# Second MLP product of a two-layer encoder written as seven block products, with one float32 arena for its raw weights

## Chip, core and metric

The kernel runs on one core of one Trainium2 chip. The metric is the device time of one execution in microseconds (us); the kernel before has three such times, 1996.44, 1997.36 and 1997.35, median 1997.35. The profile is one further execution of 1997.37 us, whose span from first to last instruction is 1995.5 us.

## What is computed

Two encoder layers on 512 tokens of width 1024, all float32. The attention mixers of a layer are left out here; the change touches what follows them:

```python
# per layer, after the first LayerNorm; h is (512, 1024)
f = jnp.square(jax.nn.relu(h @ w_ff1))                 # (512, 4096)
gate = jax.nn.sigmoid(h @ w_ple_gate)                  # (512, 1024)
u = alpha * h + f @ w_ff2 + gate * (p @ w_ple)
h = layer_norm(u, ln2_g, ln2_b)
```

Every product is made of three matrix products of rounded parts: each float32 operand is written as hi + lo, hi being a copy rounded to the matmul's type (fp32r) and lo the remainder, and the product is hi·hi + lo·hi + hi·lo.

## The kernel before

Weights arrive in chunks of 128 x 1024 float32 (512 KB), in the order in which `plan_layer` lists them. `take(key)` hands out the next chunk and first calls `ahead`, which issues loads on the SP queue (`load`, L142, two raw buffers), and splits chunks a few places ahead of their use (`split_next`, L152): ScalarE (ACT) copies raw to hi (L106), GpSimd (POOL) subtracts to get lo (L170). hi and lo live in an arena `R` of 64 slots of 128 x 512; 16 of them hold the hi and lo of h. `manual_schedule` keeps every engine's instructions in the order in which the program emits them, so an instruction that waits holds up all that stand behind it on its engine.

The MLP runs in three groups of 12, 12 and 8 inner tiles (`FF_GROUPS`). For each inner tile j of a group 24 matmuls (128 x 128 stationary, 128 x 512 moving) make 128 rows of the hidden layer for all 512 tokens in one PSUM bank. Then ACT takes relu (L1291), VectorE (DVE) squares (L1293), ACT copies to hi (L106) and DVE subtracts to lo (L109). After a group, `outer` makes its part of the second product, for each half f of the 1024 columns: four PSUM banks, one for each 128 tokens; each chunk of `w_ff2` holds two inner tiles and costs 4 x 6 matmuls. At the end of a half DVE adds the four banks into the rows `FD` (L1305, or L1303 with the factor alpha).

```python
            for c in range(4):
                n = 0
                for li, wi in SEQ3:
                    for k in range(2):
                        P.mm(P.PS[:, bs[c], :], xs(c, li, 2 * i + k), ww[k][wi], i == 0 and n == 0,
                             i == len(keys) - 1 and n == 5)
                        n += 1
```

Ahead of the MLP stands `outer` for the first column half of the gate product (chunks `pg` 0, tensor `in_wPG`), behind it the second half: there the four `pg` chunks are all taken first, and each 128 tokens then make 24 matmuls that run through all four chunks' hi before any lo. The gains g and b of the second LayerNorm (`gb`) are loaded on POOL's queue just ahead of these. LayerNorm itself is two DVE instructions on 128 x 1024 (L301, L303), and `ln_T` transposes its result on the PE (L97) for the next layer.

## Time and profile before

| what | before |
|---|---|
| median of three runs | 1997.35 us |
| the profiled execution, its span | 1997.37 us, 1995.5 us |
| PE (matmul) busy | 1954.3 us, 98%, 9440 instructions |
| DVE, ACT, POOL busy | 777.1, 755.2, 840.3 us |
| PE's share of the chain that ended last | 66% |

PE is the matmul engine, PEld its weight loads (they run beside the matmuls). Times in rows are us unless marked ns. A row of the timeline begins with the start and the length; `x` is a count, and what stands in brackets is the engine's idle time before it and what ended that. `PEclk` is the granted clock of TensorE as a share of 2.4 GHz.

### The profile page before, as it was taken

Reading aid. Unit: us, or ns where it says so; the run is one execution under the profiler, and the core shown is the slowest. Engines: PE = TensorE matmul, PEld = TensorE weight load, DVE = VectorE, ACT = ScalarE, POOL = GpSimd, SP = SyncE. Lnnn points to the kernel's source line nnn. Section 1 sums busy time; section 2 is a strip of 40 time slices with the busy share of each in tenths; the row PEclk is TensorE's granted clock in tenths of the full one; section 3 lists DMA queues with packets and bytes.
Section 4 is the critical chain, followed back from the end, with each engine's and each line's share of the span. In section 5 each row is a group of like instructions: output and inputs, shape, how many; then the busy total and the mean of one; then the engine's idle time right before and its main releaser. Section 6 shows DMA issues by size and latency. Waiting matters only on the chain.

```text
span 1995.5 us, 24072 instructions
## 1 busy us (share of the span) xinstructions
PE 1954.3 (98%) x9440; PEld 1611.4 (81%) x9440; DVE 777.1 (39%) x1565; ACT 755.2 (38%) x1313; POOL 840.3 (42%) x407
## 2 busy tenths in 40 slices
...
GB/s 168 108 54 82 99 112 97 89 82 61 147 117 95 96 126 74 107 87 103 122 111 68 57 82 103 82 125 72 101 56 168 96 102 101 102 84 127 67 120 78
DMA packets 59697, 195.96 MB, mean 98 GB/s; under 512 B 6720, under 2 KB 11968, under 8 KB 59584
## 3 DMA queue, kind: packets, MB, share of 16 engines
...
## 4 chain that ended last, share of the span: by engine, by line
PE 66%; DVE 3%; ACT 1%; POOL 1%; DMA 1%; issue 1%; DVEq 0%; ACTq 0%; POOLq 0%
PE PS L94 64%; PE PS L97 2%; ACT R L106 1%; POOL R L170 1%; DVE R L109 1%; DMA raw<-in_wO_dram 0%; DMA raw<-in_wPL_dram 0%; DVE gate L1254 0%; DVE FD L303 0%; DVE FD L301 0%; DVE p L394 0%; ACT p L386 0%; DVE qf L916 0%; DVE ysum L421 0%; DVE rt L915 0%
## 5 line engine op out<-in xcount | busy, mean ns | idle before, releaser
L94 PE MATMUL PS<-R 128*128 128x512 f32 (+4 forms) x8528 | 1886.2, 378 | 12.3 <-DVE R L365 5.3
L94 PEld LDWEIGHTS PS<-R 128*128 128x128 f32 (+1 forms) x8528 | 1508.5, 187 | 333.0 <-issue 37.6
L170 POOL TENSOR_TENSOR R<-raw,R 128x1024 fp32r<-128x1024 f32 (+1 forms) x304 | 734.7, 2421 | 848.5 <-ACT R L106 811.2
L106 ACT ACTIVATE R<-raw 128x1024 fp32r<-128x1024 f32 x306 | 321.1, 1053 | 340.8 <-PE PS L94 143.5
L106 ACT ACTIVATE R<-PS 128x128 fp32r<-128x128 f32 (+5 forms) x300 | 131.7, 450 | 131.9 <-PE PS L97 82.3
L109 DVE TENSOR_TENSOR R<-PS,R 128x512 fp32r<-128x512 f32 (+5 forms) x276 | 134.4, 494 | 118.7 <-ACT R L106 117.5
L1109 POOL TENSOR_TENSOR M<-M,gate 128x512 f32<-128x512 f32 x48 | 62.1, 1293 | 191.7 <-DVE gate L1108 135.5
L386 ACT ACTIVATE p<-p,s 128x256 f32<-128x256 f32 (+2 forms) x96 | 66.1, 688 | 187.1 <-DVE s L551 65.4
L1293 DVE TENSOR_TENSOR ff<-relu 128x512 f32<-128x512 f32 x64 | 44.3, 692 | 222.1 <-ACT relu L1291 222.1
L1305 DVE TENSOR_TENSOR FD<-FD,PS 128x512 f32<-128x512 f32 x40 | 27.5, 687 | 242.5 <-PE PS L94 242.5
L1291 ACT ACTIVATE relu<-PS 128x512 f32<-128x512 f32 x64 | 38.3, 599 | 168.5 <-PE PS L94 168.5
L394 DVE TENSOR_SCALAR p<-p,s 128x512 f32<-128x512 f32 (+3 forms) x128 | 95.0, 742 | 4.5
L97 PE MATMUL PS<-ident,p 128*128 128x128 f32 x480 | 73.6, 273 | 2.8 <-DVE p L394 1.7
L97 PEld LDWEIGHTS PS<-ident,p 128*128 128x128 f32 x480 | 58.6, 140 | 16.1 <-DVE p L394 2.5
L109 DVE TENSOR_TENSOR R<-ff,R 128x512 fp32r<-128x512 f32 x64 | 44.3, 692 | 47.6 <-ACT R L106 47.6
L1108 DVE SCALAR_TENSOR_TENSOR gate<-gate,PS 128x512 f32<-128x512 f32 x48 | 32.9, 686 | 71.1 <-ACT gate L1104 42.8
L106 ACT ACTIVATE R<-ff 128x512 fp32r<-128x512 f32 x64 | 40.5, 632 | 50.9 <-DVE ff L1293 50.9
L393 DVE RECIPROCAL s<-s 128x1 f32<-128x1 f32 x128 | 20.9, 163 | 79.3 <-ACT p L386 78.1
L277 POOL TENSOR_TENSOR s<-s,mhalf 128x1 f32<-128x1 f32 x18 | 21.4, 1192 | 71.9 <-DVE s L275 71.9
L627 DVE CUSTOM_DVE_ANT_0 p<-PS,bd 128x512 f32<-128x512 f32 x32 | 21.8, 682 | 76.1 <-PE PS L94 76.1
L386 ACT ACTIVATE p<-PS,s 128x512 f32<-128x512 f32 x32 | 22.0, 689 | 53.2 <-DVE s L481 53.0
L106 ACT ACTIVATE R<-M 128x512 fp32r<-128x512 f32 (+3 forms) x20 | 13.8, 695 | 62.3 <-POOL M L1109 52.7
...
## 6 DMA issues: line engine op xcount, KB each, us to landing
raw<-in_wF_dram SPq DMA_DIRECT2D x128, 512.0 KB, 3.4
raw<-in_wT_dram SPq DMA_DIRECT2D x106, 512.0 KB, 3.5
raw<-in_wBR_dram SPq DMA_DIRECT2D x16, 512.0 KB, 3.5
raw<-in_wO_dram SPq DMA_DIRECT2D x16, 512.0 KB, 3.6
raw<-in_wPG_dram SPq DMA_DIRECT2D x16, 512.0 KB, 3.4
raw<-in_wVD_dram SPq DMA_DIRECT2D x12, 512.0 KB, 3.4
hsp<-FD SPq DMA_DIRECT2D x8, 512.0 KB, 6.1
FD<-hsp SPq DMA_DIRECT2D x8, 512.0 KB, 5.9
```

What stands on the lines that cost most here:

```text
L94: self.nc.tensor.matmul(out, l, r, start=start, stop=stop, skip_group_check=True)
L97: self.nc.tensor.transpose(out, in_, self.ident)
L106: self.nc.scalar.activation(out=out, in_=in_, func=AF.Copy, scale=scale)
L109: self.nc.vector.tensor_tensor(out=out, in0=a, in1=hi.bitcast(F32), op=ALU.subtract)
L170: nc.gpsimd.tensor_tensor(out=lo, in0=raw, in1=hi.bitcast(F32), op=ALU.subtract)
L386: P.nc.scalar.activation(out=pt[:, 0:n], in_=src, func=AF.Exp, bias=nm, scale=1.0, accum_out=den)
L394: nc.vector.tensor_scalar(out=pt[:, 0:n], in0=pt[:, 0:n], scalar1=rd, scalar2=0.5, op0=ALU.mult, op1=ALU.mult)
L1108: nc.vector.scalar_tensor_tensor(out=t, in0=t, scalar=1.0, in1=pb, op0=ALU.add, op1=ALU.mult)
L1109: nc.gpsimd.tensor_tensor(out=P.M[:, j, :], in0=P.M[:, j, :], in1=t, op=ALU.add)
L1291: nc.scalar.activation(out=r, in_=ps, func=AF.Relu)
L1293: nc.vector.tensor_tensor(out=f, in0=r, in1=r, op=ALU.mult)
L1305: nc.vector.tensor_tensor(out=u, in0=u, in1=ps, op=ALU.add)
```

## The change

Two inner tiles (a pair), two halves of the tokens (256 each) and two halves of the columns (512 each) make a 2 x 2 by 2 x 2 block product A·W, which Strassen's scheme in Winograd's form does with seven block products instead of eight:

- left operands: a11, a12, a22, S1 = a21 + a22, S2 = S1 − a11, S3 = a11 − a21, S4 = a12 − S2;
- right operands: the four blocks of the raw weights, T1 = w12 − w11, T2 = w22 − T1, T3 = w22 − w12, T4 = T2 − w21, formed in place in the raw buffers by DVE (L196), so each T must wait until the block that it overwrites has been split;
- each right operand, 128 x 512, is now a chunk of its own: an ACT copy to hi and a POOL subtraction to lo (L201), seven in place of two chunks of 128 x 1024 per pair;
- products in the order P1, P5, P6, P2, P3, P7, P4, for all pairs of a group each; three pairs of PSUM banks X, Y, Z. P6 and P7 add to what P1 left in X, P3 to Y and P4 to Z. DVE adds X, Y or Z into `FD` after each product (L1434, L1436), so these running sums never need a further addition: P1's X must have been read before P6 goes on with it.

A product of one pair is 2 token tiles x 3 matmuls. The hidden tiles are made two at a time (`hidden`): two relu, two squares, then one split of the raw blocks, four additions on 128 x 256, one split of 128 x 1024 and one of 128 x 256. The 16 pairs of a layer go in groups of 2, 3, 3, 3, 3, 2; the first pair of the next group is made just ahead of a group's products. All former float32 buffers become one tile `F` of 39 units of 128 x 256; outside the MLP two raw buffers stay, inside it there is room for seven, and both raw halves of a pair stay from P1 until T3 or T4 have been split. Loads go up to four chunks ahead in place of two (`depth`). From P6 of the last group on, all but the two are closed again.

```diff
+U_P, U_PG, U_YS, U_RAW, N_UNIT = 16, 25, 29, 31, 39
...
-        self.M = const.tile([128, 8, 512], F32, name="M")
+        self.F = const.tile([128, N_UNIT, 256], F32, name="F")
+        self.M = self.F[:, 0:16, :].rearrange("p (a b) c -> p a (b c)", b=2)
+        self.pt = [self.units(U_P + 3 * i, 3) for i in range(3)]
+        self.pi = 0
+        self.ysum = self.units(U_YS, 2)
+        self.pg = self.units(U_PG, 4).rearrange("p (c t) -> p c t", c=4)
+        self.fa = Arena(N_UNIT)
+        self.fa.close(0, U_RAW)
...
-            self.load(self.cs + 2)
+            self.load(self.cs + self.depth)
...
+            if c['src'] is None:
+                self.cd += 1
+                continue
             if self.cd < 4:
                 c['raw'] = self.M[:, 2 * self.cd:2 * self.cd + 2, :].rearrange("p a b -> p (a b)")
             else:
-                c['raw'] = self.raw_p.tile([128, 1024], F32, tag="raw", name="raw")
+                if self.fa.find(4) is None:
+                    assert self.cd > self.cs
+                    return
+                c['u'] = self.fa.alloc(4)
+                c['raw'] = self.units(c['u'], 4)
             self.nc.sync.dma_start(out=c['raw'][:, 0:c['n']], in_=c['src'])
+            if c['quad']:
+                self.raws[c['quad'][:-1] + (c['half'],)] = c['raw'], c['u']
             self.cd += 1
+
+    def split_quad(self, c):
+
+        nc = self.nc
+        *q, what = c['quad']
+        (r0, u0), (r1, u1) = [self.raws.get(tuple(q) + (f,), (None, None)) for f in range(2)]
+        at = {'11': (r0, 0), '21': (r0, 512), '12': (r1, 0), '22': (r1, 512)}
+        b = lambda n: at[n][0][:, at[n][1]:at[n][1] + 512]
+        op = {'T1': ('11', '12', '11'), 'T2': ('11', '22', '11'), 'T3': ('12', '22', '12'), 'T4': ('21', '11', '21')}
+        src = what
+        if what in op:
+            src, x, y = op[what]
+            nc.vector.tensor_tensor(out=b(src), in0=b(x), in1=b(y), op=ALU.subtract)
+        c['k'] = 1
+        c['s'] = [self.ar.alloc(1) for _ in range(2)]
+        c['hi'], c['lo'] = [self.R[:, s, :] for s in c['s']]
+        self.acopy(c['hi'], b(src))
+        nc.gpsimd.tensor_tensor(out=c['lo'], in0=b(src), in1=c['hi'].bitcast(F32), op=ALU.subtract)
+        if what == 'T3':
+            self.fa.release(u1, 4)
+        elif what == 'T4':
+            self.fa.release(u0, 4)
...
+        if c['quad']:
+            self.split_quad(c)
+            self.cs += 1
+            return
...
-FF_GROUPS = ((0, 12), (12, 24), (24, 32))
+FF_GROUPS = (2, 3, 3, 3, 3, 2)
+FF_LOOK = {'1': (2, 1, 4), '2': (5, 1, 4)}
+PRODUCTS = (('P1', '11'), ('P5', 'T1'), ('P6', 'T2'), ('P2', '21'), ('P3', '22'), ('P7', 'T3'), ('P4', 'T4'))
+def ff_order():
+    out, a = [], 0
+    for n in FF_GROUPS:
+        out += [('1', i) for i in range(a + bool(a), a + n)]
+        if a + n < 16:
+            out.append(('1', a + n))
+        out.append(('2', range(a, a + n)))
+        a += n
+    return out
...
-    for j0, j1 in FF_GROUPS:
-        for j in range(j0, j1):
-            P.plan((l, 'f1', j), a['wF1'][l, j], 1024)
-        for f in range(2):
-            for i in range(j0 // 2, j1 // 2):
-                P.plan((l, 'f2', f, i), a['wF2'][l, f, i], 1024)
+    for what, i in ff_order():
+        if what == '1':
+            for j in (2 * i, 2 * i + 1):
+                P.plan((l, 'f1', j), a['wF1'][l, j], 1024)
+            continue
+        for prod, right in PRODUCTS:
+            for q in i:
+                f = {'P1': 0, 'P5': 1}.get(prod)
+                P.plan((l, 'f2', prod, q), None if f is None else a['wF2'][l, f, q], 1024, quad=(l, q, right), half=f)
...
-    for gi, (j0, j1) in enumerate(FF_GROUPS):
-        fs = []
-        for j in range(j0, j1):
-            w = P.take((l, 'f1', j))
-            ps = P.PS[:, P.bank(), :]
+    P.fa.close(0, 8, False)
+    P.fa.close(U_P, U_RAW - U_P, False)
+    P.depth, P.more = 4, 16
+    P.look, P.extra, P.reserve = FF_LOOK['1']
+    left = {}
+    def hidden(i):
+        f = P.bias_p.tile([128, 1024], F32, tag="bias", name="ff").rearrange("p (x t) -> p x t", x=2)
+        for x in range(2):
+            w = P.take((l, 'f1', 2 * i + x))
+            ps = P.PS[:, 5 + x, :]
             for _ in P.gemm_T(ps, w, 8, P.h_xs()):
                 pass
             P.done(w)
             r = P.tmp("relu")
             nc.scalar.activation(out=r, in_=ps, func=AF.Relu)
-            f = P.tmp("ff")
-            nc.vector.tensor_tensor(out=f, in0=r, in1=r, op=ALU.mult)
-            s = P.ar.alloc(1), P.ar.alloc(1)
-            fs.append(s)
-            P.split(P.R[:, s[0], :], P.R[:, s[1], :], f)
-        if gi == len(FF_GROUPS) - 1:
-            P.extra, P.more = 2, 9
-        for f in range(2):
-            def end(c, ps, f=f):
-                u = rows(P)[:, c, 512 * f:512 * f + 512]
-                if gi == 0 and f == 1:
+            nc.vector.tensor_tensor(out=f[:, x, :], in0=r, in1=r, op=ALU.mult)
+        s = [P.ar.alloc(n) for n in (1, 1, 2, 2, 1)]
+        R2 = lambda k: P.slot(s[k], 1).rearrange("p a (b t) -> p (a b) t", b=2)
+        P.split(R2(0), R2(1), f[:, :, 0:256])
+        S = P.bias_p.tile([128, 1024], F32, tag="bias", name="fs").rearrange("p (x t) -> p x t", x=4)
+        a11, a12, a21, a22 = f[:, 0, 0:256], f[:, 1, 0:256], f[:, 0, 256:512], f[:, 1, 256:512]
+        tt = nc.vector.tensor_tensor
+        tt(out=S[:, 0], in0=a21, in1=a22, op=ALU.add)
+        tt(out=S[:, 1], in0=S[:, 0], in1=a11, op=ALU.subtract)
+        tt(out=S[:, 2], in0=a11, in1=a21, op=ALU.subtract)
+        tt(out=S[:, 3], in0=a12, in1=S[:, 1], op=ALU.subtract)
+        S4 = lambda k: P.slot(s[k], 2).rearrange("p a (b t) -> p (a b) t", b=2)
+        P.split(S4(2), S4(3), S)
+        P.split(R2(4)[:, 0], R2(4)[:, 1], a22)
+        d = {'s': s}
+        for k, p in ((0, 'P1'), (1, 'P2')):
+            d[p] = R2(0)[:, k], R2(1)[:, k]
+        for k, p in enumerate(('P5', 'P6', 'P7', 'P3')):
+            d[p] = S4(2)[:, k], S4(3)[:, k]
+        d['P4'] = R2(4)[:, 0], R2(4)[:, 1]
+        left[i] = d
+    banks = {'X': (0, 1), 'Y': (2, 3), 'Z': (4, 7)}
+    where = {'P1': 'X', 'P6': 'X', 'P7': 'X', 'P5': 'Y', 'P3': 'Y', 'P2': 'Z', 'P4': 'Z'}
+    lo, hi, both = slice(0, 512), slice(512, 1024), slice(0, 1024)
+    gets = {'P1': (0, lo), 'P5': (1, hi), 'P6': (0, hi), 'P2': (0, lo), 'P3': (0, hi), 'P7': (1, both), 'P4': (1, lo)}
+    def second(pairs):
+        first = pairs[0] == 0
+        for prod, _ in PRODUCTS:
+            if prod == 'P6' and pairs[-1] == 15:
+                P.fa.close(0, U_RAW)
+            bs = banks[where[prod]]
+            fresh = prod in ('P1', 'P5', 'P2', 'P4')
+            for q in pairs:
+                w = P.take((l, 'f2', prod, q))
+                ww = w['hi'], w['lo']
+                for t in range(2):
+                    for n, (li, wi) in enumerate(SEQ3):
+                        P.mm(P.PS[:, bs[t], :], left[q][prod][li][:, 128 * t:128 * t + 128], ww[wi],
+                             fresh and q == pairs[0] and n == 0, q == pairs[-1] and n == 2)
+                P.done(w)
+                s = left[q]['s']
+                for k, n in {'P2': ((0, 1), (1, 1)), 'P7': ((2, 2), (3, 2)), 'P4': ((4, 1),)}.get(prod, ()):
+                    P.ar.release(s[k], n)
+            half, x = gets[prod]
+            for t in range(2):
+                ps = P.PS[:, bs[t], :]
+                u = rows(P)[:, 2 * half + t, x]
+                if prod == 'P7':
+                    u = u.rearrange("p (x t) -> p x t", x=2)
+                    ps = bass.AP(ps.tensor, ps.offset, [list(ps.ap[0]), [0, 2], [1, 512]])
+                if first and prod in ('P5', 'P6'):
                     nc.vector.scalar_tensor_tensor(out=u, in0=u, scalar=ALPHA, in1=ps, op0=ALU.mult, op1=ALU.add)
                 else:
-                    nc.vector.tensor_tensor(out=u, in0=u, in1=ps, op=ALU.add)
-            outer([(l, 'f2', f, i) for i in range(j0 // 2, j1 // 2)],
-                  lambda c, li, k: P.R[:, fs[k][li], 128 * c:128 * c + 128], end)
-        for s in fs:
-            P.ar.release(s[0], 1)
-            P.ar.release(s[1], 1)
+                    nc.vector.tensor_tensor(out=u, in0=u, in1=ps, op=ALU.subtract if prod == 'P4' else ALU.add)
+    for what, i in ff_order():
+        if what == '1':
+            hidden(i)
+            continue
+        P.look, P.extra, P.reserve = FF_LOOK['2']
+        second(i)
+        P.look, P.extra, P.reserve = FF_LOOK['1']
+    P.depth, P.more = 2, 9
```

What moves on the engines is seen in three places. First DVE, at the end of the hidden tiles of a group and the start of its products, before (second layer-0 group; `R<-ff` is the split of a hidden tile, L1305 the eviction of a finished half):

```order
L1293 TENSOR_TENSOR ff<-relu 128x512
L109 TENSOR_TENSOR R<-ff,R 128x512
L1305 TENSOR_TENSOR FD<-FD,PS 128x512 x8
L1293 TENSOR_TENSOR ff<-relu 128x512
L109 TENSOR_TENSOR R<-ff,R 128x512
```

and with the change, the same engine in a group of three pairs (`fs` holds S1 to S4; L196 forms the T blocks, here the three T2; the six L1436 are the evictions of P1, P5 and P6):

```order
L1380 TENSOR_TENSOR ff<-relu 128x512
L133 TENSOR_TENSOR R<-ff,R 128x512
L1387 TENSOR_TENSOR fs<-ff 128x256
L1388 TENSOR_TENSOR fs<-fs,ff 128x256
L1389 TENSOR_TENSOR fs<-ff 128x256
L1390 TENSOR_TENSOR fs<-ff,fs 128x256
L133 TENSOR_TENSOR R<-fs,R 128x1024
L133 TENSOR_TENSOR R<-ff,R 128x256
L196 TENSOR_TENSOR F<-F 128x512 x3
L1436 TENSOR_TENSOR FD<-FD,PS 128x512 x6
L196 TENSOR_TENSOR F<-F 128x512 x3
```

The evictions now stand behind eleven other instructions that begin only when the last hidden tile is there.

Second, DVE in the first group of a layer, which has two pairs (with what each waits for; the first L196 is T1 of the second pair, the next two are T2 of both, then come the evictions of P1 and P5):

```order
L133 TENSOR_TENSOR R<-ff,R 128x256 [waits PE_49,Activation_49]
L196 TENSOR_TENSOR F<-F 128x512 [waits DMAHW2_49,DMAHW0_49,Pool_49]
L196 TENSOR_TENSOR F<-F 128x512 [waits Pool_49] x2
L1436 TENSOR_TENSOR FD<-FD,PS 128x512 [waits PE_49] x2
L1434 SCALAR_TENSOR_TENSOR FD<-FD,PS 128x512 [waits PE_49] x2
```

Here even T1, which P5 of this very group needs, stands behind the split of the hidden pair.

Third, the SP queue at the end of the MLP, before (`raw` buffers are free as soon as POOL has split the chunk two places earlier):

```order
L149 DMA raw<-in_wF_dram 128x1024 [waits DMAHW6_49,Pool_49]
L149 DMA raw<-in_wPG_dram 128x1024 [waits DMAHW7_49,Pool_49]
L149 DMA raw<-in_wPG_dram 128x1024 [waits DMAHW0_49,Pool_49]
L149 DMA raw<-in_wPG_dram 128x1024 [waits DMAHW1_49,Pool_49]
L149 DMA raw<-in_wPG_dram 128x1024 [waits DMAHW2_49,Pool_49]
```

and with the change (the first two rows are the raw halves of the last two pairs):

```order
L180 DMA F<-in_wF_dram 128x1024 [waits DMAHW0_49]
L180 DMA F<-in_wF_dram 128x1024 [waits DMAHW1_49]
L180 DMA F<-in_wPG_dram 128x1024 [waits DMAHW5_49,DMAHW4_49,Pool_49]
L180 DMA F<-in_wPG_dram 128x1024 [waits DMAHW2_49]
L180 DMA F<-in_wPG_dram 128x1024 [waits DMAHW3_49,DMAHW1_49,Pool_49]
```

The `pg` loads now go into the two raw buffers that stay, and the units of both reach into the place of a raw half of the last pairs (the one loaded for P1 of pair 14), which is held until its T4 has been split.

## Rows read from the trace of the kernel before

**Rows 1.** The page: span, and part 1, busy time by engine.

```profile
span 1995.5 us, 24072 instructions
...
PE 1954.3 (98%) x9440; PEld 1611.4 (81%) x9440; DVE 777.1 (39%) x1565; ACT 755.2 (38%) x1313; POOL 840.3 (42%) x407
```

**Rows 2.** Busy time by stretch: length, PE, PEld, DVE, ACT, POOL; layer 0's MLP.

```profile
630.00:980.00 350.00, 350.00 (x1546) 289.82 (x1545) 63.89 (x94) 107.96 (x133) 161.84 (x69) 1.00 0.31 101
```

**Rows 3.** Timeline of DVE: evictions of two column halves of the second product.

```profile
725.32 0.69 DVE L1305 TENSOR_TENSOR FD<-FD,PS 128x512 f32<-128x512 f32 x1 [25.73 <-PE PS L94]
...
729.39 0.69 DVE L1305 TENSOR_TENSOR FD<-FD,PS 128x512 f32<-128x512 f32 x1 [0.67 <-PE PS L94]
...
757.96 0.69 DVE L1303 SCALAR_TENSOR_TENSOR FD<-FD,PS 128x512 f32<-128x512 f32 x1 [27.87 <-PE PS L94]
```

**Rows 4.** Timeline of ACT and DVE: relu, square and split of one hidden tile.

```profile
636.91 0.60 ACT L1291 ACTIVATE relu<-PS 128x512 f32<-128x512 f32 x1 [3.89 <-PE PS L94]
637.55 0.69 DVE L1293 TENSOR_TENSOR ff<-relu 128x512 f32<-128x512 f32 x1 [4.02 <-ACT relu L1291]
...
638.94 0.69 DVE L109 TENSOR_TENSOR R<-ff,R 128x512 fp32r<-128x512 f32 x1 [0.70 <-ACT R L106]
```

**Rows 5.** Groups by line and shape: count, busy us, mean ns, idle before.

```profile
L170 POOL TENSOR_TENSOR R<-raw,R 128x1024 fp32r<-128x1024 f32 x301 | 728.6, 2425 | 846.3 <-ACT R L106 809.1 <-issue 17.4 <-PE PS L94 15.8
L1109 POOL TENSOR_TENSOR M<-M,gate 128x512 f32<-128x512 f32 x48 | 62.1, 1293 | 191.7 <-DVE gate L1108 135.5 <-DVE s L393 47.8 <-PE PS L94 8.4
L106 ACT ACTIVATE R<-raw 128x1024 fp32r<-128x1024 f32 x303 | 318.3, 1055 | 336.0 <-PE PS L94 143.5 <-DMA raw<-in_wF_dram 94.0 <-DMA raw<-in_wPG_dram 24.7
L106 ACT ACTIVATE R<-ff 128x512 fp32r<-128x512 f32 x64 | 40.5, 632 | 50.9 <-DVE ff L1293 50.9
L109 DVE TENSOR_TENSOR R<-PS,R 128x256 fp32r<-128x256 f32 x64 | 26.8, 421 | 32.0 <-ACT R L106 31.7
L117 DVE SCALAR_TENSOR_TENSOR R<-raw,R 128x1024 fp32r<-128x1024 f32 x2 | 2.4, 1219 | 0.0
```

**Rows 6.** Timeline of POOL and DVE around 600 us, both reading SBUF.

```profile
599.54 6.62 POOL L170 TENSOR_TENSOR R<-raw,R 128x1024 fp32r<-128x1024 f32 x2
...
599.27 1.28 DVE L303 SCALAR_TENSOR_TENSOR FD<-FD,s,gb 128x1024 f32<-128x1024 f32 x1
...
601.67 2.24 DVE L301 SCALAR_TENSOR_TENSOR FD<-FD,s,gb 128x1024 f32<-128x1024 f32 x1
604.01 3.24 DVE L303 SCALAR_TENSOR_TENSOR FD<-FD,s,gb 128x1024 f32<-128x1024 f32 x1
```

**Rows 7.** Views of tiles M and FD: duration in ns, min/median/max, first and last start.

```profile
L1254 DVE SCALAR_TENSOR_TENSOR gate<-gate,M x16: 691/692/2875, 628.0 to 1987.0; 128x512 f32<-128x512 f32 x16
...
L1305 DVE TENSOR_TENSOR FD<-FD,PS x40: 686/687/689, 725.3 to 1964.6; 128x512 f32<-128x512 f32 x40
```

**Rows 8.** Timeline of ACT: hi copies of the last pg chunks; then part 6.

```profile
959.29 1.06 ACT L106 ACTIVATE R<-raw 128x1024 fp32r<-128x1024 f32 x1 [3.58 <-DMA raw<-in_wPG_dram]
961.91 1.06 ACT L106 ACTIVATE R<-raw 128x1024 fp32r<-128x1024 f32 x1 [1.56 <-DMA raw<-in_wPG_dram]
...
966.38 1.06 ACT L106 ACTIVATE R<-raw 128x1024 fp32r<-128x1024 f32 x1 [3.41 <-DMA raw<-in_wPG_dram]
...
raw<-in_wPG_dram SPq DMA_DIRECT2D x16, 512.0 KB, 3.4
```

**Rows 9.** Timeline of PE: two waits, each with the granted clock of the stretch behind it.

```profile
157.34 8.70 PE L94 MATMUL PS<-R 128*128 128x256 f32 x28 [2.69 <-DVE R L365]
...
158.50:162.00 3.50, 3.50 (x10) 2.71 (x9) 0.89 (x4) 1.45 (x5) 0.00 (x0) 0.52 0.46 169
...
1004.69 1.09 PE L97 MATMUL PS<-ident,FD 128*128 128x128 f32 x8 [1.75 <-DVE FD L303]
...
1006.00:1010.00 4.00, 4.00 (x29) 4.00 (x28) 3.93 (x6) 2.16 (x5) 0.88 (x1) 1.00 0.24 66
```

52 lines of the change are left out of this document (32 added, 20 removed).

## Prediction

> **What bounds the kernel now.** I read the page's head first: PE is busy for 98% of a span of 1995.5 us [rows 1]. A share is an average, so I then took the MLP of layer 0 alone: PE is busy for all 350 of its 350 us, POOL for 162 and DVE for 64 [rows 2]. Nothing but the number of matmuls sets this stage. What one costs is read from the evictions behind it, since the ends of matmuls are modelled: the first banks of two column halves are ready 757.96 − 725.32 = 32.64 us apart, with 6 chunks of 24 matmuls between [rows 3], so 32.64 / 144 = 0.2267 us each. The hidden tiles run at the same pace: 24 make 5.44 us. The change takes work from the engine that is the bound and gives more to the three that wait on it; the question is what that does to their lead.
>
> **What it removes.** A pair of inner tiles costs 48 matmuls in the second product now and 7 x 6 = 42 after. With 16 pairs and two layers that is 192 fewer, 192 x 0.2267 = **43.5 us**. The order of PE's instructions shows this many fewer, so that the change does not do what it says is excluded.
>
> **What it adds, per pair.** POOL: seven subtractions of 128x512 at 1.293 us in place of two of 128x1024 at 2.425 [rows 5], 9.05 for 4.85 us; with the two hidden-layer chunks 13.9 us. ACT: seven copies at 0.632 for two at 1.055 [rows 5], covered by ACT's idle time. DVE: four T at about 0.69 (as a square, [rows 4]), four additions of 128x256 at 0.42, a subtraction of 128x1024 at 1.22 (the nearest rows, [rows 5]), the two squares and two smaller subtractions: about 8.2 us beside the evictions. PE needs 10.88 + 42 x 0.2267 = 20.4 us for a pair, so each engine alone would fit. What does not fit is the order, in four places.
>
> **1. P6 waits for P1's eviction (groups of three pairs, four per layer).** P6 adds to the bank that P1 left, so DVE must have read it. PE comes to P6 6 chunks x 6 x 0.2267 = 8.16 us after the last hidden tile. On DVE this eviction stands behind the whole split of that tile and three T2. The chain: relu 0.60, square 0.69, copy 0.63, subtraction 0.69 (start to start the first three take 638.94 − 636.91 = 2.03 [rows 4], so the hand-offs cost little), additions 4 x 0.42, copy of 128x1024 1.06, subtraction 1.22, subtraction 0.42, three T2 2.07, eviction 0.69 [rows 3]: 9.75, with some 0.2 for hand-offs 9.95. So PE waits 1.8 us in each of these groups even if nobody disturbs DVE. I take 3.0 (the reason follows in 5): 12 us per layer, between 7 and 20.
>
> **2. The first group has two pairs, so less time.** T1 of its second pair stands on DVE behind the same split: it ends at 7.0 + 0.2 + 0.7 = 7.9, its hi is there at 8.6, its lo at 9.9, and PE wants it after 3 chunks, at 4.1. The second T2 waits for that lo (its place is overwritten), to 10.6; P1's eviction ends at 11.3, and P6, due at 5.44, starts then. **6 us** per layer, between 4 and 8.
>
> **3. The last group** uses a pair right after making it: its hi and lo for P1 come at 2.0 and 2.7 (due at 1.36), those of S1 at 5.6 and 6.8. **2.5 us** per layer; between 0, if the split runs ahead, and 5.
>
> **4. The gate weights behind the MLP.** Before, their hi copies lie within the second product, the last at 966.38 [rows 8], where PE never waits [rows 2]. Now the first two loads wait until T4 of pair 14 has been split. After the last hidden tile's split (7.2) DVE evicts P1 and P5 (to 9.4), forms two T3 (10.8), evicts P6, which PE ends at 10.75 (12.2), and forms T4 (12.9); with the copy, 0.63, and POOL, that has some of its queue to finish, this is over at about 15.7. PE wants the gate weights at 10.75 + 8 x 1.36 = 21.6. From there each buffer is a chain of a landing at 3.4 [rows 8], copy 1.06, POOL 2.4: the third and fourth chunks' hi come at 27.2 and 29.6, and PE needs all four for its first eight matmuls. It waits 4.7 and 1.9 us: **7 us** per layer, between 3 and 10. The 3.5 us per chunk agree with the 7.1 us that two took before (959.29 to 966.38, [rows 8]).
>
> **5. POOL and DVE get in each other's way.** Near 600 us DVE and POOL take turns: two POOL subtractions last 6.62 instead of 4.8 us, and DVE's 1.28 becomes 2.24 and 3.24 [rows 6]. An instruction with two SBUF inputs (L1254) usually takes 0.69 and once 2.88 us; L1305, with one input in PSUM, never more than 0.689 [rows 7]. All of DVE's new instructions have two SBUF inputs. Five turns took from 599.27 to 607.25, 7.98 us, where the single lengths add to 8.64 [rows 6], so 0.92 of the sum. Here the sum is 13.9 + 8.2 = 22.1 us per pair, hence 20.4 when fully interleaved: as much as PE has. So POOL still has a subtraction or two to make when the split of the last hidden tile begins, and each costs that chain up to 1.2 us: this is the 1.2 between 1.8 and 3.0 in place 1.
>
> The Trainium skill has the rule in "SBUF — State Buffer", section "Who interferes with whom": a DVE instruction with two SBUF inputs contends with a GpSimd instruction that reads SBUF, and whoever issues first holds the shared port for the whole instruction. The trace agrees (2.88 against 0.689 us). Taken strictly, 22.1 us per pair is a floor above PE's 20.4; that is the second rival below.
>
> **6. The clock.** A PE wait of 2.69 us was followed by 3.5 us at a granted clock of 0.52, that is at 1.2 GHz; one of 1.75 us by full speed [rows 9]. A fall costs 3.5 x 0.48 = 1.7 us. Places 2 and 4 wait longer than 2.69: two falls, 3.4 us per layer, between 0 and 8.
>
> **The sum.** 12 + 6 + 2.5 + 7 + 3.4 = 31 us per layer, 62 in all, against 43.5 saved: +18.5. The profiled execution took 1997.37 us, 0.02 above the median of 1997.35, so no correction: **2016 us**. The rest of the program changes names and places of buffers only. The lower ends give 14 per layer, 28 − 43.5 = −15.5, 1982; the upper ones 51, 102 − 43.5 = +58.5, 2056. About 4 us (0.2%) is what a measurement can tell from no change.
>
> **Rivals.**
> - *The lead holds, faster.* If DVE reaches P1's eviction within 8.16 us, place 1 is gone; this needs 1.8 us less than I count, for instance if hand-offs overlap the instructions. With place 2 at 4, place 4 at 3 and no clock falls: 14 − 43.5 = −29.5, **1968**. For it: PE's queue is full before and a pair's work fits each engine. Against it: the chain is a sum of measured lengths, and the order leaves no way around it. 0.22.
> - *POOL and DVE become the bound, slower still.* If their turns cost the full 22.1 per pair, a group of three takes 66.2 instead of 61.2. Four groups lose 20, the first 6, the last 4, the gate weights, behind a late POOL, 9, the clock 4: 43 per layer, 86 − 43.5 = +42.5, **2040**. It decides from 20.4 us of shared time per pair. For it: the 2.88; against it: the 0.92. 0.17.
> - *It cancels.* No contention and no clock: 6 + 7.2 + 2.5 + 6.6 = 22.3 per layer, 44.6 − 43.5 = +1, **1998.5**. 0.13.
>
> **The numbers.** My forecast has 0.48. Faster by over 0.2% is the first rival and a little of the forecast's lower edge, 0.23; within 0.2% the third, 0.12; slower 0.65. The range runs from 1980, leaving out most of the first rival, to 2050, above the second.
>
> **What would show it.** PE busy should fall by some 43 us and PE idle in the MLP rise from none to some 60, in the places named: waits on L1436 of 1.8 us or more before P6, five per layer; one on ACT of about 4.5 in each first group; two at the gate product, on ACT copies of `in_wPG` chunks. POOL's 128x512 subtractions beside T instructions should last over 1.5 us, DVE's T and squares show maxima near 2 where the trace before has 0.69. I am wrong if PE stays at full share through the groups of three: then the chain in place 1 is shorter than its parts. I am also wrong if POOL is busy throughout and PE waits for its lo copies: then the second rival holds.

## The result, and the profile after

The changed kernel takes **2063.55 us** (median of four, 2063.39 to 2066.01) against 1997.36 us for the kernel before in the same session: 1.0334 times, 95% interval 1.0321 to 1.0346, slower by 66.2 us. The forecast was slower, 2016 us; the result lies above its range.

The page of the changed kernel, beside [rows 1]:

```profile
span 2064.2 us, 24765 instructions
...
PE 1948.2 (94%) x9248; PEld 1594.8 (77%) x9248; DVE 1143.9 (55%) x1973; ACT 842.8 (41%) x1505; POOL 1014.2 (49%) x567
```

192 matmuls fewer, yet PE's busy time fell by 6.1 us in place of 43.5, and PE's idle time rose from 41.2 to 116.0. −6.1 + 74.8 = +68.7 is the difference of the two spans. So there are two things to find: 74.8 us of waits, and 37.4 us by which the remaining matmuls became slower.

PE's waits in layer 0's MLP, in the timeline of PE (layer 1 has the same within 0.6 us each):

```profile
672.73 3.43 PE L118 MATMUL PS<-R 128*128 128x512 f32 x6 [4.25 <-ACT R L130]
...
736.93 63.09 PE L118 MATMUL PS<-R 128*128 128x512 f32 x270 [4.60 <-ACT R L130]
804.92 63.08 PE L118 MATMUL PS<-R 128*128 128x512 f32 x270 [4.90 <-ACT R L130]
873.33 63.14 PE L118 MATMUL PS<-R 128*128 128x512 f32 x270 [5.32 <-ACT R L130]
941.50 34.50 PE L118 MATMUL PS<-R 128*128 128x512 f32 x144 [5.04 <-ACT R L130]
980.69 21.09 PE L118 MATMUL PS<-R 128*128 128x512 f32 x80 [4.69 <-ACT R L130]
1002.01 0.73 PE L118 MATMUL PS<-R 128*128 128x512 f32 x2 [0.23 <-ACT R L130]
1007.94 1.22 PE L118 MATMUL PS<-R 128*128 128x512 f32 x2 [5.20 <-ACT R L130]
1011.06 17.96 PE L118 MATMUL PS<-R 128*128 128x512 f32 x66 [1.90 <-ACT R L130]
```

The first is the first group (place 2), the next four stand before P6 in the groups of three (place 1), then come the last group (place 3) and the gate product (place 4). Between these places PE works without a break. The view puts the waits before P6 down to an ACT copy; the times speak for an eviction: P1's first eviction (L1436, below) starts at 736.11 and ends at 736.78, P6 starts 0.15 us later. In the later run m2_dvelo, where the copies of T2 are done 2.6 us earlier, P6 starts 0.14 us after that eviction too.

The slower matmuls stand right behind the waits. Windows of PE: length, busy time and matmuls, granted clock:

```profile
736.00:742.00 6.00, 5.07 (x15) 0.72 0.00 0
...
980.00:988.00 8.00, 7.31 (x20) 0.62 0.00 0
1007.00:1018.00 11.00, 8.16 (x21) 0.55 0.43 133
```

In the first, PE resumes at 736.93 and makes 15 matmuls in 5.07 us where 22 would fit. Matmul starts are 0.43 us apart for 3.4 us, then 0.2267 again: 1.2 GHz, then 2.4.

In what follows, **lost** means this: over all matmuls of a stretch, what their distances from start to start exceed 0.2267 us, summed. The changed kernel loses 54.3 us in layer 0's MLP and 54.1 in layer 1's; 108.4 − 43.5 = +64.9, near the measured 66.2 (68.7 between the two profiled spans). By place: first group 8.1, groups of three 6.5, 6.8, 7.3 and 7.0, last group 7.7, gate product 10.9.

Why the waits before P6 are 5 us and not 1.8 is seen on DVE, ACT and POOL ahead of the first of them (timeline of the changed kernel, one part per engine):

```profile
722.33 0.68 DVE L196 TENSOR_TENSOR F<-F 128x512 f32<-128x512 f32 x1
724.21 1.40 DVE L1380 TENSOR_TENSOR ff<-relu 128x512 f32<-128x512 f32 x1 [1.19 <-ACT relu L1379]
725.53 0.68 DVE L196 TENSOR_TENSOR F<-F 128x512 f32<-128x512 f32 x1
727.39 1.39 DVE L1380 TENSOR_TENSOR ff<-relu 128x512 f32<-128x512 f32 x1 [1.18 <-ACT relu L1379]
...
736.11 2.47 DVE L1436 TENSOR_TENSOR FD<-FD,PS 128x512 f32<-128x512 f32 x4
...
714.87 0.58 ACT L1379 ACTIVATE relu<-PS 128x512 f32<-128x512 f32 x1
...
723.05 0.63 ACT L130 ACTIVATE R<-F 128x512 fp32r<-128x512 f32 x1 [1.92 <-DVE F L196]
723.59 0.58 ACT L1379 ACTIVATE relu<-PS 128x512 f32<-128x512 f32 x1
726.24 0.63 ACT L130 ACTIVATE R<-F 128x512 fp32r<-128x512 f32 x1 [2.07 <-DVE F L196]
726.78 0.58 ACT L1379 ACTIVATE relu<-PS 128x512 f32<-128x512 f32 x1
...
723.76 1.29 POOL L201 TENSOR_TENSOR R<-F,R 128x512 fp32r<-128x512 f32 x1 [7.43 <-ACT R L130]
726.95 1.28 POOL L201 TENSOR_TENSOR R<-F,R 128x512 fp32r<-128x512 f32 x1 [1.89 <-PE PS L118]
...
721.74 10.59 PE L118 MATMUL PS<-R 128*128 128x512 f32 x46
```

PE works until 721.74 + 10.59 = 732.33; the last 36 of these matmuls are P1 and P5, so the last hidden tile ended at 732.33 − 36 x 0.2267 = 724.17. Its relu starts only at 726.78, **2.6 us late**: on ACT it stands behind the copy of a T block, the copy behind T on DVE, T behind the first tile's square, the square behind the first tile's relu, and that one behind another T's copy. And these squares last 1.40 us in place of 0.69: the copy's end lets POOL start the block's lo, and the relu that follows on ACT lets DVE start the square 0.45 us later, so in both the two meet. The lateness grows, because this round takes longer than PE: from the second relu of a pair to that of the next it is 726.78 − 714.87 = 11.91 us, and PE makes a pair in 10.88. From the relu on the chain is the predicted one: P6 starts 10.15 us later, against 9.95 worked out (0.7 more for the square, 0.5 less for the other links together), and 2.61 + 10.15 − 8.16 = 4.60.

### The profile page after: what moved, and what is told of

It is laid out like the page before. It is cut to its first block, busy times and chain, and to the rows that moved or that the text cites. A ratio compares the mean times of both kernels' runs of the same rounds, so it can differ in the third digit from the quotient of the medians.

```text
span 2064.2 us, 24765 instructions
## 1 busy us (share of the span) xinstructions
PE 1948.2 (94%) x9248; PEld 1594.8 (77%) x9248; DVE 1143.9 (55%) x1973; ACT 842.8 (41%) x1505; POOL 1014.2 (49%) x567
## 4 chain that ended last, share of the span: by engine, by line
PE 77%; DVE 11%; ACT 6%; issue 3%; DMA 2%; POOL 1%; SPq 0%; DVEq 0%; ACTq 0%; POOLq 0%
PE PS L118 73%; ACT R L130 4%; PE PS L121 3%; DVE R L133 3%; DVE F L196 2%; DVE ff L1380 1%; POOL R L201 1%; DMA F<-in_wF_dram 1%; DMA F<-in_wPG_dram 1%; ACT relu L1379 1%; DVE fs L1387 0%; DMA F<-in_wCQ_dram 0%; ACT F L448 0%; DVE FD L1436 0%; DVE FD L365 0%
## 5 line engine op out<-in xcount | busy, mean ns | idle before, releaser
L118 PE MATMUL PS<-R 128*128 128x512 f32 (+6 forms) x8336 | 1880.4, 383 | 85.5 <-ACT R L130 74.5
L118 PEld LDWEIGHTS PS<-R 128*128 128x128 f32 (+2 forms) x8336 | 1491.7, 190 | 417.2 <-ACT R L130 86.4
L230 POOL TENSOR_TENSOR R<-F,R 128x1024 fp32r<-128x1024 f32 (+1 forms) x243 | 589.4, 2437 | 525.5 <-ACT R L130 487.8
L130 ACT ACTIVATE R<-F 128x1024 fp32r<-128x1024 f32 (+2 forms) x502 | 408.8, 836 | 466.9 <-DVE F L196 197.6
L201 POOL TENSOR_TENSOR R<-F,R 128x512 fp32r<-128x512 f32 x224 | 326.8, 1488 | 236.8 <-ACT R L130 220.2
L196 DVE TENSOR_TENSOR F<-F 128x512 f32<-128x512 f32 x128 | 142.1, 1146 | 18.0 <-DMA F<-in_wF_dram 14.6
L448 ACT ACTIVATE F<-F,s 128x256 f32<-128x256 f32 (+2 forms) x96 | 66.1, 688 | 188.5 <-DVE s L611 66.5
L1436 DVE TENSOR_TENSOR FD<-FD,PS 128x512 f32<-128x512 f32 (+1 forms) x160 | 114.7, 758 | 41.6 <-PE PS L118 41.6
L456 DVE TENSOR_SCALAR F<-F,s 128x512 f32<-128x512 f32 (+3 forms) x128 | 95.0, 742 | 4.5
L121 PE MATMUL PS<-ident,F 128*128 128x128 f32 x504 | 78.7, 273 | 5.6 <-DVE F L456 1.7
L121 PEld LDWEIGHTS PS<-ident,F 128*128 128x128 f32 x504 | 61.5, 140 | 20.3 <-DVE F L456 2.5
```

The lines of the kernel that those rows point to most:

```text
L118: self.nc.tensor.matmul(out, l, r, start=start, stop=stop, skip_group_check=True)
L121: self.nc.tensor.transpose(out, in_, self.ident)
L130: self.nc.scalar.activation(out=out, in_=in_, func=AF.Copy, scale=scale)
L196: nc.vector.tensor_tensor(out=b(src), in0=b(x), in1=b(y), op=ALU.subtract)
L201: nc.gpsimd.tensor_tensor(out=c['lo'], in0=b(src), in1=c['hi'].bitcast(F32), op=ALU.subtract)
L230: nc.gpsimd.tensor_tensor(out=lo, in0=raw, in1=hi.bitcast(F32), op=ALU.subtract)
```

## Experiments

All are compared with 2063.5 us unless a base is named. Theory A: the order of instructions on DVE and ACT makes the waits. Rival B: DVE and POOL, sharing the SBUF, have too much to do.

### Order or sharing: a square of four kernels

**e4_relu** edits the order alone: chunks ahead are split behind a hidden tile's relu.

```diff
-        self.ahead(self.ci, self.ci + self.look, self.ci + self.more)
+        if on or self.cs <= self.ci:
+            self.ahead(self.ci, self.ci + self.look, self.ci + self.more)
...
-            w = P.take((l, 'f1', 2 * i + x))
+            first = True
+            w = P.take((l, 'f1', 2 * i + x), not first)
...
             nc.scalar.activation(out=r, in_=ps, func=AF.Relu)
+            if first:
+                P.ahead(P.ci - 1, P.ci - 1 + P.look, P.ci - 1 + P.more)
```

> The T instructions, copies and subtractions of chunks ahead that a hidden tile's take emits are emitted behind that tile's relu instead of ahead of its matmuls; nothing is removed. In the changed kernel the last hidden tile of a group of three ends on PE at about 724.2 us (46 matmuls from 721.74, of which the last 36 are P1 and P5), its relu begins only at 726.78, behind the ACT copy of a T block. Theory A, made sharper: these 2.6 us are part of the wait before P6. Then each of the eight waits falls from 5.0 to about 2.4 us, and some half-speed stretches get shorter: 2063.5 - 21 to 29 = 2035 to 2043 us. Rival B (the shared SBUF sets the wait): no change, 2058 to 2068 us.

Measured **2030.31 us**, 33 less. **c1_psum** changes the sharing alone:

```diff
-            nc.vector.tensor_tensor(out=f[:, x, :], in0=r, in1=r, op=ALU.mult)
+            nc.vector.scalar_tensor_tensor(out=f[:, x, :], in0=ps, scalar=0.0, in1=r, op0=ALU.max, op1=ALU.mult)
```

> The changed kernel with one edit: the square multiplies relu's result by max(PSUM, 0), so the same instruction stands at the same place of DVE's order but has one input in PSUM and one in SBUF, as the evictions, which never lasted longer than alone in the kernel before. If DVE and POOL taking turns on the SBUF lengthens the chain, the square falls from 1.43 us (mean) to about 0.7 and POOL's subtraction beside it from 1.49 to 1.29, the two squares in the chain give 1.4 us, each wait before P6 falls from 5.0 to about 3.6: 2063.5 - 8 x 1.4 = 2052 us, 2045 to 2056. If the square's length is not due to sharing, it stays at 1.4 and the time at 2060 to 2066. If the gain is that of e5_square (2029), the order of the square on DVE had no part in it.

Measured **2037.36 us**, 26 less. Both edits together are **c2_psum**:

> The same square on e4_relu (2030.3 us), where relus are not late and the wait before P6 is 1.74 us, the length of an undisturbed chain. If sharing matters only through late relus, nothing is left to gain: 2027 to 2032. If it also slows the chain there and POOL's pace behind P6 (1.7 us per group), 4 to 12 us less: 2018 to 2026.

Measured **2030.46 us**: the second adds nothing to the first. The timelines say why. The squares, in the view of their tile (min/median/max in ns), the relu and PE in e4_relu, with the end of the last hidden tile at 719.78 + 10.59 − 8.16 = 722.21:

```profile
L1384 DVE TENSOR_TENSOR ff<-relu x64: 675/693/7599, 635.8 to 1964.6; 128x512 f32<-128x512 f32 x64
...
722.30 0.60 ACT L1381 ACTIVATE relu<-PS 128x512 f32<-128x512 f32 x1 [1.77 <-PE PS L118]
...
719.78 10.59 PE L118 MATMUL PS<-R 128*128 128x512 f32 x46
732.10 33.07 PE L118 MATMUL PS<-R 128*128 128x512 f32 x137 [1.74 <-ACT R L130]
```

and in c1_psum, with the end at 719.67 + 13.31 − 8.16 = 724.82:

```profile
L1380 DVE SCALAR_TENSOR_TENSOR ff<-PS,relu x64: 675/692/694, 638.4 to 1972.8; 128x512 f32<-128x512 f32 x64
...
714.67 0.58 ACT L1379 ACTIVATE relu<-PS 128x512 f32<-128x512 f32 x1
...
725.28 0.58 ACT L1379 ACTIVATE relu<-PS 128x512 f32<-128x512 f32 x1
...
723.31 0.69 DVE L1380 SCALAR_TENSOR_TENSOR ff<-PS,relu 128x512 f32<-128x512 f32 x1 [1.19 <-ACT relu L1379]
...
722.87 1.30 POOL L201 TENSOR_TENSOR R<-F,R 128x512 fp32r<-128x512 f32 x1 [6.72 <-ACT R L130]
...
719.67 13.31 PE L118 MATMUL PS<-R 128*128 128x512 f32 x58
734.74 11.56 PE L118 MATMUL PS<-R 128*128 128x512 f32 x47 [1.76 <-ACT R L130]
```

In both, the relu is at most 0.5 us late and the wait is 1.74 and 1.76 us, near the 1.8 of place 1. In layer 0's four groups of three e4_relu loses 15.1 us and c1_psum 15.7, the changed kernel 27.6. So order and sharing make the other 3 us together. c1_psum leaves the order as it was: with squares 0.7 us shorter the round from relu to relu takes 725.28 − 714.67 = 10.61 us and fits into PE's 10.88. The reverse, the new order with squares still at 1.40, was not run: in e4_relu the meeting is mostly gone too (median 693), and the last pair's squares there take 0.69. So order is shown as what brings the two instructions together, not as a cause without sharing.

After these waits of 1.74 and 1.76 us the granted clock stays at 1.00 (732 to 735 us in e4_relu, 734.7 to 738 in c1_psum), as in [rows 9]. In c1_psum the square has one SBUF input and keeps its length (at most 0.694 us) beside a POOL subtraction of 1.30; in the changed kernel the same view has:

```profile
L1380 DVE TENSOR_TENSOR ff<-relu x64: 676/1396/2686, 637.9 to 1999.3; 128x512 f32<-128x512 f32 x64
```

That is what the Trainium skill says in "SBUF — State Buffer", section "Who interferes with whom": with at most one SBUF input, outside its 2-port modes, a DVE instruction does not contend with GpSimd; with two it contends with a GpSimd instruction that reads SBUF. The trace agrees.

**e5_square** has the squares on ACT, so order and sharing change together:

```diff
+            nc.scalar.activation(out=f[:, x, :], in_=r, func=AF.Square)
```

> The changed kernel with one edit: the squares of the hidden tiles on ACT in place of DVE, so two of DVE's instructions with two SBUF inputs per pair are gone (mean 1.43 us there, minimum 0.68). If sharing the SBUF with POOL lengthens the chain (place 5), each of the two squares ahead of the split gets 0.7 to 0.8 us shorter, both count, since the second relu waits behind the first square's T: the waits before P6 fall by 0.7 to 1.5 us: 2063.5 - (6 to 12) = 2051 to 2058 us. If the order alone sets the wait, the square only changes its engine (ACT 0.6 us, one hand-off less on the way to the copy): 2060 to 2066 us.

Measured **2028.75 us**, 35 less, far below both expectations: they counted the 0.7 us once per square along one wait, and did not see that the lateness builds up from pair to pair.

### The clock

**e2_fill** puts matmuls into the wait:

```diff
+            if prod == 'P6' and len(pairs) == 3:
+                for n in range(22):
+                    P.mm(P.PS[:, 5, :], P.R[:, P.hh, 0:128], P.R[:, P.hh + 1, :], True, True)
```

> 22 further matmuls per group of three (5.0 us at full speed), into a free bank and read by nobody, ahead of P6, so that PE works where it waited 4.6 to 5.3 us; everything else is as in the changed kernel. If each wait costs its own length and then a stretch at half clock (theory A), the waits are filled at no cost and only the stretches go: 3.4 to 6.8 us at 0.5, eight of them, 8.5 us lost in layer 0 and 10.2 in layer 1: 2063.5 - 18.7 = about 2045 us, with PE's records at full clock behind P6. If the half clock has another cause than the idle time, the stretches stay and the time is 2063 to 2068 us.

Measured **2061.01 us**. The stretch behind the first wait, in windows of PE (compare with 736.00:742.00 above), then POOL's timeline behind it and one later window:

```profile
736.00:742.00 6.00, 6.00 (x28) 1.00 0.01 3
...
736.20 21.95 POOL L201 TENSOR_TENSOR R<-F,R 128x512 fp32r<-128x512 f32 x15 [7.49 <-ACT R L130]
...
747.00:757.00 10.00, 9.72 (x40) 1.00 0.03 6
```

The waits and the half clock before and behind P6 are gone, as theory A has it; so the clock falls there because of the waits. But little time is won: 40 matmuls in the later window where 44 would fit. POOL makes one subtraction in 21.95 / 15 = 1.46 us, PE needs one in 6 x 0.2267 = 1.36. In the changed kernel the wait and the slow matmuls had given POOL its lead. The filler costs 88 x 0.2267 = 20.0 us per layer and what is lost in the groups, mostly to POOL's pace, about 7: nearly the 27.6 of the changed kernel. The expectation forgot this next limit.

### The waits before P6, taken away in two other ways

**e1_defer** moves the squares and the split of the pair for the next group:

```diff
+            if not later:
+                nc.vector.tensor_tensor(out=f[:, x, :], in0=r, in1=r, op=ALU.mult)
...
+            if prod == 'P5' and waiting:
+                waiting.pop()()
```

> In the four groups of three pairs, the squares and the split of the hidden pair that the group itself does not use are emitted behind P5's evictions; its relu stays. Theory A (order): P6 waits because P1's eviction stands on DVE behind that split. Then the eight waits of 4.6 to 5.3 us before P6 (about 40 us in both layers) go, and with them the eight half-speed stretches of 3.4 or 6.8 us behind them (about 19 us): 2063.5 - 59 = about 2005 us, 1998 to 2020. Rival B (DVE and POOL share the SBUF and have too much work): the same instructions still run, so the waits come back at P3, P7 or the next P1, and the time stays above 2050.

Measured **2040.10 us**, between the two expectations. The waits of 5 us are gone; in their place (timeline of PE and POOL):

```profile
739.74 0.73 PE L118 MATMUL PS<-R 128*128 128x512 f32 x2 [0.36 <-ACT R L130]
741.31 23.94 PE L118 MATMUL PS<-R 128*128 128x512 f32 x94 [0.83 <-POOL R L201]
...
739.82 14.54 POOL L201 TENSOR_TENSOR R<-F,R 128x512 fp32r<-128x512 f32 x9 [5.45 <-PE PS L118]
```

PE waits for POOL's lo, POOL needs 1.62 us each beside DVE's moved work: rival B's limit, but only once A's wait is out of the way. The four groups now lose some 17 us per layer, before 27.6.

**o1_order** only puts P2 ahead of P6:

```diff
-PRODUCTS = (('P1', '11'), ('P5', 'T1'), ('P6', 'T2'), ('P2', '21'), ('P3', '22'), ('P7', 'T3'), ('P4', 'T4'))
+PRODUCTS = (('P1', '11'), ('P5', 'T1'), ('P2', '21'), ('P6', 'T2'), ('P3', '22'), ('P7', 'T3'), ('P4', 'T4'))
```

> The changed kernel with one edit: P2 ahead of P6 (P1, P5, P2, P6, P3, P7, P4), so P6 and T2 are due three chunks, 4.1 us, later, 12.2 us after the last hidden tile in place of 8.16. The measured chain to P1's eviction is 10.0 us from the relu and the relu 2.6 late, 12.6 in all. Theory A: the waits before P6 fall from 5.0 to 0.5 us and the half-speed matmuls behind them go; of 27.3 us per layer in the four groups of three some 25 go, but POOL's pace gives back 2 to 4 us per group, as in e1: 2063.5 - 50 + (16 to 32) = 2030 to 2045 us. If POOL and DVE had a lead to build in these 4 us, nothing is given back: about 2013. If the wait is POOL's for T2 rather than DVE's for P1's eviction, it moves with T2 and is gone too, but then P2 waits: 2050 or more.

Measured **2037.83 us**, in the range of the first case, but for another reason. From the timelines of PE and of SP's loads:

```profile
732.03 0.73 PE L118 MATMUL PS<-R 128*128 128x512 f32 x2 [1.42 <-ACT R L130]
733.59 64.33 PE L118 MATMUL PS<-R 128*128 128x512 f32 x268 [0.83 <-POOL R L201]
...
959.74 31.81 SPq L180 DMA_DIRECT2D F<-in_wPG_dram  x4
```

P6 no longer waits, but P2 does: for the copy of w21, which stands on ACT behind those of the hidden pair, and for its lo. The first group of three loses 2.8 us in these two waits and 3.1 in distances of 0.34 and 0.44 us, the pace at which POOL's parts come; the four groups together lose 25.5 us per layer, so only 2 of 27.6 are won there. The rest is won in places 3 and 4: the program closes the arena at P6 of the last group, and that now comes two chunks later. The first gate load is issued at 959.74 us in place of 996.05 (below), the gate product loses 1.9 us in place of 10.9 and the last group 4.6 in place of 7.7. In layer 0 some 5 us come back as a longer wait behind the gate product. That the time fell into the expected range was luck.

### The gate weights

**e3_gate**:

```diff
-            if prod == 'P6' and pairs[-1] == 15:
-                P.fa.close(0, U_RAW)
...
     pg = [P.take((l, 'pg', 1, i)) for i in range(4)]
+    P.fa.close(0, U_RAW)
```

> The float32 arena is closed to two raw buffers only after the gate weights have been taken, not at P6 of the last group, so their loads need not wait for T4 of pair 14. If that wait is the cause (place 4 of the prediction), the two waits at the gate product (5.2 and 1.9 us, and the 0.2 ahead of them) go in both layers, with the 10.2 us at half clock behind them (5.1 lost): 2 x 12.4 = 25 us, to about 2039 us. Rival: the loads are late because the SP queue or the DMA rate holds them up (they landed in 5.2 us, before in 3.4); then the first wait stays above 3 us and the time is above 2052 us.

Measured **2044.55 us**, 19 less. SP issues the four loads, of the changed kernel and then of e3_gate:

```profile
996.05 9.74 SPq L180 DMA_DIRECT2D F<-in_wPG_dram  x4
```

```profile
961.13 32.47 SPq L180 DMA_DIRECT2D F<-in_wPG_dram  x4
...
1004.01 11.63 PE L118 MATMUL PS<-R 128*128 128x512 f32 x50 [0.47 <-POOL R L230]
```

The first begins 35 us earlier, and one wait of 0.47 us is left. The gate product loses 0.8 us in place of 10.9, twice 10 us, and this is the gain; the expected 25 had priced the half clock too high. Place 4 is shown: the loads were late because of the closed arena.

### Towards a version that gains

**l1_both** joins e3 and e4.

> The two edits that gained most, together: lookahead behind the relu (e4, -33 us) and the arena closed behind the gate weights (e3, -19 us). They touch different waits, so their gains should add: 2063.5 - 33.2 - 19.0 = 2011 us, 2006 to 2017, with 1.7 us waits before P6 and none over 1 us at the gate product. If the gate weights' gain came from another source (less work on POOL at that moment, say), the sum falls short: above 2020.

Measured **2016.74 us**, within the range but 5 us short of the sum. **l2_look** adds a longer lookahead, **l3_half** late subtractions, **l4_both** both:

```diff
-FF_LOOK = {'1': (2, 1, 4), '2': (5, 1, 4)}
+FF_LOOK = {'1': (5, 1, 4), '2': (7, 1, 4)}
...
-        P.split(S4(2), S4(3), S)
-        P.split(R2(4)[:, 0], R2(4)[:, 1], a22)
+        P.acopy(S4(2), S)
+        P.acopy(R2(4)[:, 0], a22)
...
+            if prod == 'P1' and waiting:
+                waiting.pop()()
```

> On l1_both: chunks are split up to 6 (in place of 3) ahead during hidden tiles and 8 (in place of 6) ahead during products, so most T1 and T2 stand on DVE, and their lo copies on POOL, ahead of the last hidden pair's split. Theory A (order): the wait before P6 loses two T2 (1.4 us) and its POOL lag and nearly goes, 2.0 x 4 per layer; the first group loses half of its 7.9 us; and POOL, whose subtractions pace PE behind P6 in e4 (spacings of 0.34 and 0.44 us in place of 0.227, 1.7 us per group), starts with a lead: up to 7 per layer. 2011 - 16 - 8 - (0 to 14) = 1973 to 1987 us. Rival B (POOL and DVE sharing SBUF have as much work as PE has time): a lead cannot be built, the waits only move: above 2000.

> On l1_both: of the hidden pair that the group does not use, the two last subtractions (128x1024 and 128x256, 1.64 us, behind a copy of 1.06) are emitted behind P1's evictions, in the four groups of three. Theory A: the chain to P1's eviction, 9.95 us, loses at least 1.6 and P6 is due at 8.16, so the wait of 1.74 us goes: -2.0 x 4 x 2 = -16, given back in part (0 to 1.5 us per group) because POOL then paces PE, as in e1: 1995 to 2007 us. Rival B: P6 then waits for the lo of T2 instead and nothing is gained, 2009 to 2013.

> On l1_both: the longer lookahead of l2_look and the late subtractions of l3_half, the latter in the first group too. Theory A: no wait before P6, the first group at 3 us or less, POOL with a lead; what stays is the last group (4.4 us per layer) and a little: 2011 - 16 - 10 - (6 to 14) = 1971 to 1979 us, so faster than the kernel before by about 1%. Rival B: 2000 or more, as in l2_look, since both edits only move work of POOL and DVE.

Measured **2009.88, 2007.08 and 1999.68 us**. l3_half ends at the upper end of theory A's range: its waits before P6 lose 0.55 us each in place of 2.0, and POOL's pace takes 1.9 per group in place of 1.6. In l2_look the waits before P6 stay (0.7 to 1.8 us lost), new ones come at the start of the hidden tiles, on late relus (1.3 to 1.5), and the last group loses 8.3: here rival B's number was the right one. l4_both, against before, is still not faster (1.0011, 1.0002 to 1.0020).

**m1_last** shortens the lookahead for the last pair (`if i == 15: P.look, P.extra, P.reserve = (2, 1, 4)`), **m2_dvelo** then moves two of seven lo parts to DVE, **m4_square** the squares to ACT:

> On l4_both: while the last hidden pair of a layer is made, chunks are split 3 ahead as in l1_both, not 6. In l4_both P1 of the last group waits 5.9 us because the relus of pair 15 stand on ACT behind copies of T blocks, which wait on DVE for T, and T for POOL and late loads; with the half-speed matmuls behind it the last group loses 9.4 us per layer, in l1_both 4.4. If relus behind T copies are the cause, the last group is back at about 4.4: 1999.7 - 10 = 1990 us, 1986 to 1994. If the late loads of the last two raw pairs are the cause, nothing changes: 1997 to 2001.

> On m1_last: the lo parts of the two raw blocks w21 and w22 of each pair (P2, P3) are made by DVE (128x512, 0.69 us) in place of POOL (1.29, mean 1.58 in l4_both). POOL then has 11.3 in place of 13.9 us per pair and both engines together 20.9 in place of 22.1. Rival B in its present form (POOL's subtractions pace PE behind P6, and T2 waits for POOL): the 3.3 us per layer of 0.34 and 0.44 us spacings go, and most of the 4.2 us of late relus at the start of hidden tiles: 6 to 15 us less than m1_last, so about 1980 us, 1975 to 1986. Theory A alone (only the order on DVE counts): two more DVE instructions per pair, each behind an ACT copy, delay what stands behind them: equal to m1_last or up to 10 us slower.

> On m1_last: squares on ACT as in e5_square. DVE and POOL lose 1.4 of 22.1 us of shared time per pair. If sharing costs what is left of the waits, 3 to 8 us less than m1_last; if only the order counts, no change within 2 us; if ACT becomes the one that is late (relus stand behind squares there), slower by up to 8.

```diff
+        if what in ('21', '22'):
+            self.vsub(c['lo'], b(src), c['hi'])
+        else:
+            nc.gpsimd.tensor_tensor(out=c['lo'], in0=b(src), in1=c['hi'].bitcast(F32), op=ALU.subtract)
...
-            nc.vector.tensor_tensor(out=f[:, x, :], in0=r, in1=r, op=ALU.mult)
+            nc.scalar.activation(out=f[:, x, :], in_=r, func=AF.Square)
```

Measured **1998.16, 2003.29 and 1984.95 us**. m1_last changed nothing that is clear of noise (the last group loses 8.8 us in place of 9.4), so the lookahead of that one pair is not what holds up the last group. m2_dvelo lost 5 us. PE's waits before P6 are back (1.0 to 2.4 us), two of the four:

```profile
792.51 61.90 PE L118 MATMUL PS<-R 128*128 128x512 f32 x270 [2.10 <-ACT R L130]
856.42 42.44 PE L118 MATMUL PS<-R 128*128 128x512 f32 x186 [2.01 <-ACT R L130]
```

DVE makes such a part in 0.76 us where POOL takes 1.53, but it stands in DVE's order behind an ACT copy, and P1's eviction behind it: less work in sum, a longer chain. m4_square gained 13 us, more than expected; the stops at late relus ahead of hidden tiles, which lose 1.5 to 1.8 us each in m1_last, lose 0.3 to 0.8.

**o2_order** (P2 ahead of P6 on m4_square), **o3_last** (the lookahead of the group before the last cut to 6 besides) and **r1_last** (both, for the last group alone):

> The same order of products on m4_square (1985 us). If T2 coming too early is what is left, the first group loses most of its 3.7 us per layer, the late relus 1.6, and the last group (8.4), where T2 blocks stand on ACT ahead of pair 15's relus, comes to about 4.4: 1985 - 7 - 3 - 8 = 1967 us, 1962 to 1975. If the late loads and POOL's backlog are the cause, the waits only move by three chunks: 1980 to 1986.

> o2_order, and during P7 and P4 of the group before the last the lookahead is 6 chunks in place of 8, so that no T2 of the last group is formed before pair 15's relus. If T2's copies ahead of the relus cause the last group's wait: 0 to 8 us less than o2_order, with P1's wait there below 2 us. If the late loads of raw pairs 14 and 15 do, the same as o2_order within 2 us.

> On m4_square (1985 us): in the last group of a layer alone P2 stands ahead of P6, and ahead of it no T2 is formed before pair 15's relus. In m4_square this group loses 8.4 us per layer, in o3_last, with this order in all groups, 5.2. If late relus behind T2 copies are the cause: 3 to 5 us less per layer, 1975 to 1979 us. If late loads of pairs 14 and 15 are, 1983 to 1987.

```diff
+LAST = tuple(PRODUCTS[i] for i in (0, 1, 3, 2, 4, 5, 6))
+def products(pairs):
+    return LAST if pairs[-1] == 15 else PRODUCTS
...
-        for prod, _ in PRODUCTS:
+        for prod, _ in products(pairs):
+            if prod == 'P7' and pairs[-1] == 13:
+                P.look, P.extra = 6, 0
```

Measured **1996.54, 1994.47 and 1981.59 us** (the diff is r1_last's). In o2_order the first group loses 6.5 us in place of 3.7 and each group of three some 1.2 to POOL's pace. The same edit gained 26 us in the changed kernel mainly because it let the gate loads start early; m4_square has e3's edit, so this could not be won again. Why the first group loses more was not followed up. o3_last is not clear of o2_order's noise: its last group loses 5.2 us in place of 7.2, and as much comes back behind the gate product. r1_last lies between its two expectations: the last group loses 4.1 us in place of 8.4, but 2.0 come back in each layer in the gate product, on POOL's lo, and 1.7 in layer 0 behind it. It is the fastest: **0.9918 times the kernel before, interval 0.9903 to 0.9933**. Its page, and from the timeline of PE two groups of three and the waits at the last group and behind the gate product:

```profile
PE 1917.3 (97%) x9248; PEld 1574.2 (80%) x9248; DVE 1042.2 (53%) x1909; ACT 873.2 (44%) x1569; POOL 1007.6 (51%) x567
...
767.81 61.57 PE L118 MATMUL PS<-R 128*128 128x512 f32 x270 [0.18 <-ACT relu L1390]
829.73 61.49 PE L118 MATMUL PS<-R 128*128 128x512 f32 x270 [0.35 <-ACT relu L1390]
...
945.04 0.50 PE L118 MATMUL PS<-R 128*128 128x512 f32 x1 [1.03 <-ACT R L130]
...
988.77 1.83 PE L121 MATMUL PS<-ident,FD 128*128 128x128 f32 x8 [4.52 <-DVE FD L366]
```

A group of three now takes 61.5 us, and 270 x 0.2267 = 61.2.

## Right and wrong, point by point

- **Removed work, 43.5 us:** right; r1_last, with few slow matmuls left, has PE busy 37 us less than before.
- **Place 1, wrong in size:** 3.0 us per wait taken, 4.6 to 5.3 measured, 19.9 per layer for 12, the upper end of the bounds. The undisturbed 1.8 was met by waits of 1.74 and 1.76, in part by luck: in c1_psum, with nothing lengthened, the chain from the relu takes 734.74 − 725.28 = 9.46 us, 0.5 less than the 9.95 counted, and the relu there is 0.46 late. The step that failed is "each costs that chain up to 1.2 us": sharing was charged once, at one instruction. The chain began too late: the relu itself stood behind T and its copy, and each square met a POOL subtraction (2.6 us late and 0.7 more in the chain; c1 takes nearly all of this away with the squares alone, e4 with the order, and c2 finds nothing further). The order of DVE was read as far back as the last tile's relu; ACT's order, in which the copy of T stands ahead of that relu, was not read.
- **Place 2:** 6 taken, 4.25 + 0.40 measured. Its mechanism, the split ahead of T1, was read from the order and not tried alone.
- **Place 3:** 2.5 taken, 4.69 measured: PE stops at 980.69 − 4.69 = 976.00, six matmuls of P1 behind pair 15's last tile, which so ended at 974.6; its relu starts at 977.93, 3.3 us late, as before P6.
- **Place 4:** waits of 4.7 and 1.9 taken, 5.20 and 1.90 measured, and gone in e3.
- **Place 5:** right that sharing matters, and by the row (2.88 against 0.689, [rows 7]; not "once", as the trace before has two such lengths of L1254, 2.51 and 2.88); wrong in where. The means for the changed kernel are 1.488 us for L201 and 1.431 for squares, but POOL is idle for half of the span: the second rival did not hold. Its limit shows only where A's waits are gone, at 1.46 to 1.62 us per chunk.
- **Place 6, wrong in number, the largest miss:** 1.7 us per fall was right for the four before P6 (3.4 us at half clock each). Two falls per layer were counted; there are seven, and those of the first group, the last and the gate product last 5.4 to 7 us (a granted clock of 0.62 over 8 us and 0.55 over 11 us, less the idle time in them). The text had itself put place 1 at 3.0 us, above the 2.69 of [rows 9], and counted no fall there.
- **The sum:** waits 27.5 us per layer taken and 36.5 measured; slower matmuls 3.4 taken, 18.7 measured (37.4 / 2). The larger part of the error is the second: the step "two falls, 3.4 us per layer". The seven stretches at half clock make about 16 us per layer; the other 2 to 3 are not explained.
- **What should show it:** the waits came at the places named, those at the gate product on ACT copies of its chunks (those before P6 are listed under ACT copies as well, not under L1436); squares reached 2.69 us. PE's busy time, which was to fall by 43, told at once that something else was there.
